# Seven-product pairs in the mixing stages of a two-layer encoder

## The chip, the cores and the metric

The kernel runs on one core of a Trainium2 chip. The metric is the device time of one execution in microseconds; the kernel before takes 1991.8 us, the median of three runs (1990.81, 1991.8, 1995.55). The engines are TensorE (PE, with PEld for its weight loads), VectorE (DVE), ScalarE (ACT), GpSimd (POOL) and SyncE (SP), which only issues transfers.

## The reference

Two layers work on 256 tokens of width 2048, in float32. With the parts that do not matter here left out:

```python
for l in range(DEPTH):                       # DEPTH = 2
    h = rms_norm(x, g_mix[l])
    z = h @ w_in[l]
    # layer 0: z = u (1536), v (1536), memory queries (512): gelu, spatial gating u * s(v)
    # layer 1: z = q (1536), k (512), v (512), memory queries (512): attention with axial rotary
    kv = rms_norm(mem, g_mem[l]) @ w_mem_kv[l]           # 512 keys and 512 values for 256 memory tokens
    x = x + concatenate([tok_out, mem_out]) @ w_out[l]   # 2048 x 2048
    gate, up = split(rms_norm(x, g_ffn[l]) @ w_gate_up[l])   # 2048 x 2 * 5632
    x = x + (silu(gate) * up) @ w_down[l]                # 5632 x 2048
```

## The kernel before, in words

**Products.** Each float32 operand is split into a rounded half `hi` and a residue `lo`; `matmul3` (L187, L188, L189) forms a product as three PE instructions on 128x512 pieces. Activations are kept transposed as `hi` and `lo` in a `Parts` table, 128 features by 128 tokens each. Weights arrive by transfers on SP into `raw` tiles (four of them, 128x2048), and `halves` makes `whi` on ACT (L271) and `wlo` on DVE (L272), three buffers each.

**Two schemes.** `Linear` computes 512 output columns for both token halves: 16 row blocks by 2 token halves by 3 instructions, 96 in all, in two output banks; one `tick` comes for every two row blocks, eight in all. `Pair` computes two neighbouring blocks of 512 columns at once in eight units, each of two row blocks by two token halves by two column blocks. A unit is done by `eight` (24 instructions) or by `seven`, a seven-product scheme (21 instructions). `seven` needs sums of the four weight pieces (L380, L381, L382 in `prepare`, into a tile `T`, and the residue of `T` in a second call of `halves`) and sums of the activations (`feature_sums`, `activation_sums`, L324 to L331). The products 1, 5, 6, 7 of all the sevens are collected in four banks of the room's own, which `inner` adds up into `E` after the last seven (L434 to L437); the products 2, 3, 4, 8 have the four banks of `psa`, which `outer` adds to that at the end (L458). A unit makes two ticks, a pair 16.

**Order.** The program is written as one sequence; `later(n, f)` puts a piece of work n ticks ahead, `tick` runs what is due. From that sequence a planner with a time model fixes each engine's order of instructions. Activations to be transposed go through `turned`: a copy that separates 16-bit planes (L200), a transposing transfer on ACT's queue (L201), and a copy that joins them (L206), after which `split` makes `hi` and `lo` (L181, L182).

**Stages.** Layer 0 mixes first: v in three blocks, the memory queries, `w_mem_kv` keys and values, u in three blocks, then the four blocks of `w_out` with `add_residual` (L658), all by `Linear`. Meanwhile the gates, the memory's norm and the four memory heads (`attend`: `queries`, `scores`, `turn`, `weigh`) run from `later`. Layer 1 mixes likewise with keys, values, three query blocks with attention, memory queries, memory keys and values, and `w_out`. Between lies the feed-forward: three chunks (four, four and three blocks of 512 hidden columns), each with its gate/up pairs, two or three sevens in eight units, and then two `w_down` pairs, with up to three. The mixing stage of a layer has a room of 36 tiles of 128x512 (`big`) and four single banks; the feed-forward has 26 tiles, two `T` buffers, `E`, and the four banks as two double ones.

## Time and profile before

| | |
|---|---|
| median of three runs | 1991.8 us (1990.81 to 1995.55) |
| the profiled execution | 1994.35 us, its span 1992.6 us |
| PE, DVE, ACT, POOL busy | 99%, 83%, 61%, 4% of the span |
| 128x512 products | 8457 of PE's 8913 instructions |
| read from HBM | 394.45 MB |
| granted clock of PE | 0.999 as a mean |

PE's busy time is the union of its instructions, and these overlap: what a product costs is read from the number of products in a stretch that PE fills. A stage is a stretch of the span; the view of windows gives the busy time of every engine in it.

### The profile page before, as it was taken

The numbers are of one execution on the slowest core, as the hardware profiler recorded it, in microseconds if no ns is written. First come the engines' busy times: TensorE is split into PE (matmuls) and PEld (weight loads), VectorE is DVE, ScalarE is ACT, GpSimd is POOL, SyncE is SP. The second block draws the span as 40 slices with busy tenths as digits, with TensorE's granted clock in tenths as the row PEclk, the third lists the DMA queues.
The fourth block names the chain that finished last, engine by engine and source line by source line (L and its number), as shares of the span: only waits on it lengthen the run. The fifth ranks groups of instructions, "written<-read, shape, count | busy, mean of one in ns | idle before, by whom it ended". The sixth has DMA issues, their size and how long they took to land.

```text
span 1992.6 us, 24068 instructions
## 1 busy us (share of the span) xinstructions
PE 1980.8 (99%) x8913; PEld 1640.5 (82%) x8913; DVE 1649.1 (83%) x1783; ACT 1214.7 (61%) x1461; POOL 80.1 (4%) x122
## 2 busy tenths in 40 slices
PE   9999999999999999999999999999999999999998
PEld 7888888888888888888888888888888888888877
...
GB/s 348 300 190 227 217 213 188 194 227 205 232 240 181 231 212 240 233 186 226 250 200 210 154 148 158 216 166 230 224 201 248 198 216 236 199 249 196 223 212 125
DMA packets 283494, 425.93 MB, mean 214 GB/s; under 512 B 89680, under 2 KB 89936, under 8 KB 283376
## 3 DMA queue, kind: packets, MB, share of 16 engines
...
q14 instruction: 48, 0.39, 0.1%
HBM read 394.45 MB, written 2.10 MB: 199 GB/s over the span
## 4 chain that ended last, share of the span: by engine, by line
PE 92%; DMA 3%; DVE 2%; ACT 2%; issue 1%; SPq 0%; ACTq 0%; DVEq 0%
PE acc L189 26%; PE acc L187 26%; PE acc L188 26%; PE m L187 4%; PE m L189 4%; PE m L188 4%; DMA a<-a 2%; DVE wlo L272 1%; DMA raw<-in_w_in_a 1%; ACT whi L271 1%; PE m L193 0%; DVE T L380 0%; PE m L561 0%; PE m L698 0%; ACT junk L213 0%
## 5 line engine op out<-in xcount | busy, mean ns | idle before, releaser
L272 DVE TENSOR_TENSOR wlo<-raw,whi 128x2048 fp32r<-128x2048 f32 (+2 forms) x466 | 840.8, 1821 | 209.5 <-ACT whi L271 203.3
L271 ACT CAST whi<-raw 128x2048 fp32r<-128x2048 f32 (+2 forms) x466 | 705.8, 1535 | 445.8 <-PE acc L188 313.5
L187 PE MATMUL acc<-whi,h 128*128 128x512 f32 x1440 | 561.2, 390 | 0.8 <-ACT whi L271 0.8
L188 PE MATMUL acc<-whi,h 128*128 128x512 f32 x1440 | 560.7, 389 | 0.0
L189 PE MATMUL acc<-wlo,h 128*128 128x512 f32 x1440 | 514.4, 390 | 0.2
L187 PE MATMUL acc<-whi,a 128*128 128x512 f32 x999 | 389.3, 390 | 3.5 <-ACT a L181 3.4
L188 PE MATMUL acc<-whi,a 128*128 128x512 f32 x999 | 389.7, 390 | 0.0
L189 PE MATMUL acc<-wlo,a 128*128 128x512 f32 x999 | 366.7, 391 | 0.8 <-DVE wlo L272 0.7
L189 PEld LDWEIGHTS acc<-wlo,h 128*128 128x128 f32 x1440 | 270.3, 188 | 57.8 <-DVE wlo L272 2.1
L187 PEld LDWEIGHTS acc<-whi,h 128*128 128x128 f32 x1440 | 270.5, 188 | 56.6 <-ACT whi L271 1.4
L188 PEld LDWEIGHTS acc<-whi,h 128*128 128x128 f32 x1440 | 270.4, 188 | 55.6
L187 PEld LDWEIGHTS acc<-whi,a 128*128 128x128 f32 x999 | 187.9, 188 | 42.7 <-ACT a L181 3.9
L189 PEld LDWEIGHTS acc<-wlo,a 128*128 128x128 f32 x999 | 187.8, 188 | 41.7 <-DVE wlo L272 2.8
L188 PEld LDWEIGHTS acc<-whi,a 128*128 128x128 f32 x999 | 188.0, 188 | 38.9
L271 ACT CAST whi<-T 128x1536 fp32r<-128x1536 f32 x93 | 137.8, 1481 | 122.6 <-PE acc L188 103.3
L272 DVE TENSOR_TENSOR wlo<-T,whi 128x1536 fp32r<-128x1536 f32 x93 | 162.9, 1751 | 1.8 <-ACT whi L271 1.8
L380 DVE TENSOR_TENSOR T<-raw 128x1024 f32<-128x1024 f32 x93 | 113.4, 1220 | 20.6 <-DMA raw<-in_w_gate_up 20.4
L187 PE MATMUL m<-whi,a 128*128 128x512 f32 x284 | 110.7, 390 | 0.0
L188 PE MATMUL m<-whi,a 128*128 128x512 f32 x284 | 110.5, 389 | 0.0
L189 PE MATMUL m<-wlo,a 128*128 128x512 f32 x284 | 110.5, 389 | 0.0
L458 DVE TENSOR_TENSOR e<-acc,e 128x512 f32<-128x512 f32 x120 | 78.8, 684 | 2.0 <-PE acc L189 1.7
L206 ACT COPY sg<-a 128x1024 uint16<-128x1024 uint16 x44 | 51.5, 1171 | 33.1 <-DMA a<-a 32.8
(145 smaller groups left out, 1517.7 us busy)
## 6 DMA issues: line engine op xcount, KB each, us to landing
...
```

The source lines that it names most:

```text
L187: nc.tensor.matmul(out, lhsT=a[0], rhs=b[0], start=start, stop=False)
L188: nc.tensor.matmul(out, lhsT=a[1], rhs=b[0], start=False, stop=False)
L189: nc.tensor.matmul(out, lhsT=a[0], rhs=b[1], start=False, stop=stop)
L206: copy(halves, back.rearrange("p (h n) -> p n h", h=2))
L271: nc.scalar.copy(hi[:, cut], raw[:, cut])
L272: nc.vector.tensor_tensor(lo[:, cut], raw[:, cut], hi[:, cut].bitcast(F32), ALU.subtract)
L380: nc.vector.tensor_tensor(T[:, :2], raw[:, 1:4:2], w01, ALU.add)
L458: nc.vector.tensor_tensor(o[t][n], self.bank[name], o[t][n], op)
```

## The change

Six pairs of linear blocks become `Pair`s in which units 0 and 1 have seven products: v blocks 1 and 2, memory keys and values of layer 0, u blocks 0 and 1, keys and values of layer 1, and blocks 0 and 1 of `w_out` in both layers (`two`). The activation sums come from `block_sums`, put ahead with `sums_later`; the first of them in three places uses the `T` buffer as scratch (`apart`). Layer 0's room has 29 tiles beside one `T` and one `E`; in layer 1 the sums lie in separate tiles (`loose`) of `big` or `kept`. The four banks change between single and double with `open_banks`. The first v block is copied out of its banks. The memory heads of layer 0 run later (waits 4, 30, 34, 40 for 4, 16, 20, 28), the u blocks' plane copies go from DVE to ACT, and layer 1's keys are turned later. In the last chunk of `w_down` the seven-product units stand one or two places later, and the last activations are collected three ticks after their transfer for two. `feature_sums` gives way to `block_sums`, which does the same.

```diff
...
 KC4 = 4
-MIX_TILES = 36
+MIX_TILES = (29, 36)
 FFN_TILES = 26
...
     def __init__(self):
-        self.ap, self.whole = {}, {}
+        self.ap, self.whole, self.pair = {}, {}, {}
...
-    def open_rooms(scope, name, tiles, banks):
+    def open_rooms(scope, name, tiles, banks, scratch=2):
         room["p"] = scope.enter_context(tc.tile_pool(name=name, bufs=tiles, reuse_waits="tile"))
-        room["m"] = scope.enter_context(tc.tile_pool(name=f"ps_{name}", bufs=4 // banks, space=PS))
+        room["scratch"] = scratch
+        open_banks(name, banks)
+    def open_banks(name, banks):
+        close_banks()
+        room["psum"] = ExitStack()
+        room["m"] = room["psum"].enter_context(tc.tile_pool(name=nm(f"ps_{name}"), bufs=4 // banks, space=PS))
         room["banks"] = banks
+    def close_banks():
+        if "psum" in room:
+            room.pop("psum").close()
...
-    def split(src, shape):
-        hi = big(F32R, shape)
-        lo = big(F32R, shape)
+    def split(src, shape, tiles=None):
+        hi, lo = [(tiles or big)(F32R, shape) for _ in range(2)]
         nc.scalar.copy(hi, src)
...
                 parts.put(2 * i + c, t, hi[:, c, ts], lo[:, c, ts])
+        parts.pair[i] = hi, lo
...
             nc.vector.tensor_tensor(lo[:, cut], raw[:, cut], hi[:, cut].bitcast(F32), ALU.subtract)
+        return [(hi[:, c, :], lo[:, c, :]) for c in range(n)]
+    def single_halves(raws):
+        n = len(raws)
+        hi = wp.tile([P, KC4, NB], F32R, tag="whi", name=nm("whi"))[:, :n]
+        lo = wp.tile([P, KC4, NB], F32R, tag="wlo", name=nm("wlo"))[:, :n]
+        for c, raw in enumerate(raws):
+            nc.scalar.copy(hi[:, c], raw)
+            nc.vector.tensor_tensor(lo[:, c], raw, hi[:, c].bitcast(F32), ALU.subtract)
         return [(hi[:, c, :], lo[:, c, :]) for c in range(n)]
...
-    def activation_sums(a0, a1, apart=False):
+    def activation_sums(a0, a1, apart=False, tiles=None):
         if apart:
-            q = room["p"].tile([P, KC3, NB], F32, tag="T", name=nm("T"), bufs=2)[:, 0].rearrange("p (c n) -> p c n", n=P)
+            q = room["p"].tile([P, KC3, NB], F32, tag="T", name=nm("T"), bufs=room["scratch"])[:, 0].rearrange("p (c n) -> p c n", n=P)
         else:
-            q = big(F32, [P, 4, P])
+            q = (tiles or big)(F32, [P, 4, P])
         nc.vector.tensor_tensor(q[:, 0], a1[:, 0], a1[:, 1], ALU.subtract)
...
         else:
-            hi, lo = split(q, [P, 4, P])
+            hi, lo = split(q, [P, 4, P], tiles)
         return [(hi[:, i, :], lo[:, i, :]) for i in range(4)]
...
-        def __init__(self, parts, sums, w, na, nb, order, fast, into=None, onto=None):
+        def __init__(self, parts, sums, w, na, nb, order, fast, into=None, onto=None, loose=None):
             self.parts, self.sums, self.w, self.na, self.nb = parts, sums, w, na, nb
-            self.into, self.onto = into, onto
+            self.into, self.onto, self.loose = into, onto, loose
             self.bank, self.two, self.part, self.ready = {}, {}, {}, {}
...
             if i in self.fast:
-                T = room["p"].tile([P, KC3, NB], F32, tag="T", name=nm("T"), bufs=2)
-                w01 = raw[:, 0].unsqueeze(1).to_broadcast([P, 2, NB])
-                nc.vector.tensor_tensor(T[:, :2], raw[:, 1:4:2], w01, ALU.add)
-                nc.vector.tensor_tensor(raw[:, 0], T[:, 0], raw[:, 3], ALU.add)
-                nc.vector.tensor_tensor(T[:, 2], raw[:, 0], raw[:, 2], ALU.add)
+                if self.loose:
+                    T = [self.loose(F32, [P, NB]) for _ in range(KC3)]
+                    for c in range(2):
+                        nc.vector.tensor_tensor(T[c], raw[:, 1 + 2 * c], raw[:, 0], ALU.add)
+                else:
+                    T = room["p"].tile([P, KC3, NB], F32, tag="T", name=nm("T"), bufs=room["scratch"])
+                    w01 = raw[:, 0].unsqueeze(1).to_broadcast([P, 2, NB])
+                    nc.vector.tensor_tensor(T[:, :2], raw[:, 1:4:2], w01, ALU.add)
+                t0, t2 = (T[0], T[2]) if self.loose else (T[:, 0], T[:, 2])
+                nc.vector.tensor_tensor(raw[:, 0], t0, raw[:, 3], ALU.add)
+                nc.vector.tensor_tensor(t2, raw[:, 0], raw[:, 2], ALU.add)
                 self.ready[i] = raw, T
...
             t2, w00, w10, w11 = halves(raw, KC4)
-            t1, t3, t4 = halves(T, KC3)
+            t1, t3, t4 = single_halves(T) if self.loose else halves(T, KC3)
             get, (q5, s2, q7, q3) = self.parts.get, self.sums[i]
...
             b = self.bank
+            if self.loose:
+                e = [self.loose(F32, [P, NB]) for _ in range(4)]
+                nc.scalar.copy(e[0], b[1])
+                nc.vector.tensor_tensor(e[3], b[6], e[0], ALU.subtract)
+                for one, name in ((1, 5), (2, 7)):
+                    nc.vector.tensor_tensor(e[one], b[name], e[3], ALU.add)
+                nc.vector.tensor_tensor(e[3], b[5], e[2], ALU.add)
+                self.out = [[e[2 * t + n] for n in range(2)] for t in range(NT)]
+                return
             E = room["p"].tile([P, 4, NB], F32, tag="e", name=nm("e"), bufs=1)
...
             hi, lo = split(po.rearrange("p (h s) -> p h s", h=2), [P, 2, S])
+            parts.pair[kc0 // 2 + pr] = hi, lo
             for hh in range(2):
...
-        def keys(self):
-            acc = linear(self.parts, w_mem_kv[self.l], 0)
+        def keys(self, acc=None):
+            acc = acc or linear(self.parts, w_mem_kv[self.l], 0)
             kn = head_norm(acc, self.r, ghead[f"mk{self.l}"])
...
-        def values(self):
-            self.V = scaled(linear(self.parts, w_mem_kv[self.l], NB), self.r)
+        def values(self, acc=None):
+            self.V = scaled(acc or linear(self.parts, w_mem_kv[self.l], NB), self.r)
...
+    def block_sums(parts, i, apart=False, tiles=None):
+        whole = []
+        for t in range(NT):
+            if i in parts.pair:
+                both = [a[:, :, t * P:(t + 1) * P] for a in parts.pair[i]]
+            else:
+                both = [a[:, 2 * (i % 2):2 * (i % 2) + 2] for a in parts.whole[i // 2, t]]
+            a = (tiles or big)(F32, [P, 2, P])
+            nc.vector.tensor_tensor(a, both[0].bitcast(F32), both[1].bitcast(F32), ALU.add)
+            whole.append(a)
+        return activation_sums(*whole, apart, tiles)
+    def two(parts, sums, w, n0, order, fast, loose=None):
+        g = Pair(parts, sums, w, n0, n0 + NB, order, fast, loose=loose)
+        g.run()
+        return [[g.out[t][n] for t in range(NT)] for n in range(2)]
+    def sums_later(parts, sums, i, wait, apart=False, tiles=None):
+        def make():
+            sums[i] = block_sums(parts, i, apart, tiles)
+        later(wait, make)
     hT = Parts()
...
         scope = ExitStack()
-        open_rooms(scope, f"mix{l}", MIX_TILES, 1)
+        open_rooms(scope, f"mix{l}", MIX_TILES[l], 2, 1)
         cat = Parts()
         m = Memory(l)
+        hsums, msums, csums = {}, {}, {}
         if l == 0:
...
                     hi, lo = split(whole, [P, 4, P])
+                    cat.whole[c, t] = hi, lo
                     for i in range(4):
...
-                turned(us, 3, parts, True, nc.vector.tensor_copy)
+                turned(us, 3, parts, True)
...
                 for t in range(NT):
-                    v[t][c] = big()
+                    v[t][c] = acc[t] if not c else big()
                     nc.scalar.activation(v[t][c], acc[t], AF.Gelu, scale=norm.r[t])
...
-            later(7, lambda: gated(0, acc))
-            for c in (1, 2):
-                gated(c, linear(hT, w, TOK + c * NB))
+            whole = [big() for _ in range(NT)]
+            for t in range(NT):
+                nc.vector.tensor_copy(whole[t], acc[t])
+            later(7, lambda: gated(0, whole))
+            for i in range(2):
+                sums_later(hT, hsums, i, 1 + 2 * i, not i)
+            for c, acc_c in zip((1, 2), two(hT, hsums, w, TOK + NB, (2, 3, 0, 4, 1, 5, 6, 7), (0, 1))):
+                gated(c, acc_c)
+            open_banks("mix0", 1)
             for t in range(NT):
...
                     later(3 + 3 * t + c, lambda t=t, c=c: gate(t, c))
-            m.attend(linear(hT, w, 2 * TOK), norm.r, cat, (4, 16, 20, 28), True)
-            m.keys()
-            m.values()
+            for i in range(2):
+                sums_later(m.parts, msums, i, 4 + 2 * i, not i)
+            m.attend(linear(hT, w, 2 * TOK), norm.r, cat, (4, 30, 34, 40), True)
+            open_banks("mix0", 2)
+            keys, values = two(m.parts, msums, w_mem_kv[0], 0, (2, 3, 4, 0, 5, 1, 6, 7), (0, 1))
+            open_banks("mix0", 1)
+            m.keys(keys)
+            m.values(values)
+            open_banks("mix0", 2)
+            for i in range(2):
+                sums_later(hT, hsums, i, i, not i)
+            blocks = two(hT, hsums, w, 0, (2, 3, 0, 4, 1, 5, 6, 7), (0, 1))
             for c in range(3):
-                acc = linear(hT, w, c * NB)
+                acc = blocks[c] if c < 2 else linear(hT, w, c * NB)
+                if c == 2:
+                    for i in range(2):
+                        sums_later(cat, csums, i, 1 + 2 * i)
                 for t in range(NT):
...
             m.prep(20, 2)
-            acc = linear(hT, w, TOK)
+            for i in range(2):
+                sums_later(hT, hsums, i, 1 + 2 * i)
+            acc, values = two(hT, hsums, w, TOK, (2, 3, 4, 0, 5, 1, 6, 7), (0, 1), big)
+            open_banks("mix1", 1)
             kn = head_norm(acc, norm.r, ghead["k"], True)
...
-            later(7, turn_k)
-            own["v"] = scaled(linear(hT, w, TOK + MEMW), norm.r)
+            own["v"] = scaled(values, norm.r)
+            later(3, turn_k)
             for c in range(3):
...
         units = kd if l else [(12, KC4), (0, KC4), (4, KC4), (8, KC4)]
+        if l:
+            for i in range(2):
+                sums_later(cat, csums, i, 1 + 2 * i, tiles=kept)
+            later(6, lambda: open_banks("mix1", 2))
+            blocks = two(cat, csums, w_out[l], 0, (2, 3, 4, 0, 5, 1, 6, 7), (0, 1), kept)
+        else:
+            blocks = two(cat, csums, w_out[l], 0, (2, 3, 0, 1, 6, 7, 4, 5), (0, 1))
         for j in range(4):
-            acc = linear(cat, w_out[l], j * NB, units)
+            acc = blocks[j] if j < 2 else linear(cat, w_out[l], j * NB, units)
             add_residual(acc, j, norm, gslice("ffn", l), hF, j < 3, nc.scalar.copy if l else nc.vector.tensor_copy)
+        close_banks()
         room.clear()
...
-        def feature_sums(i):
-            j, c = i // 2, 2 * (i % 2)
-            whole = []
-            for t in range(NT):
-                hi, lo = hF.whole[j, t]
-                a = big(F32, [P, 2, P])
-                nc.vector.tensor_tensor(a, hi[:, c:c + 2].bitcast(F32), lo[:, c:c + 2].bitcast(F32), ALU.add)
-                whole.append(a)
-            sums[i] = activation_sums(*whole)
         for i in fast:
-            later(2 + 2 * i, lambda i=i: feature_sums(i))
+            sums_later(hF, sums, i, 2 + 2 * i)
...
                     nc.vector.scalar_tensor_tensor(a, g.out[t][1], norm.r[t], a, ALU.mult, ALU.mult)
-                    wait, ticks = (3, 2) if f == chunk[-1] else (11, 3)
+                    wait, ticks = (3, 3 if last else 2) if f == chunk[-1] else (11, 3)
                     later(wait + t, lambda a=a, t=t, f=f, ticks=ticks: turn_a(a, t, f, ticks))
...
                 for n, i in enumerate(some):
-                    order.insert((0, 2, 4 + (not jj))[n], i)
+                    order.insert(1 + n + jj if last else (0, 2, 4 + (not jj))[n], i)
                 into = [Columns(X2[t][jj]) for t in range(NT)] if last else None
...
         norm = next_norm
+        close_banks()
         room.clear()
...
     flush()
```

## The prediction

> **What bounds the kernel now.** I first read the page's busy shares and the list of what TensorE (PE) waited for.
>
> ```profile
> PE 1980.8 (99%) x8913; PEld 1640.5 (82%) x8913; DVE 1649.1 (83%) x1783; ACT 1214.7 (61%) x1461; POOL 80.1 (4%) x122
> ```
>
> ```profile
> PE acc L187 <- ACT a L181: 3.4, 1, 3.4
> ```
>
> PE is busy for all but 12 us of the span of 1992.6 us, and the longest of its waits is one of 3.4 us. A PE that does not wait is shortened only by taking products away; so the question is what one product costs, and whether VectorE (DVE), the next engine at 83%, can deliver the operands of the new scheme in time. Both are read stage by stage. I found the stages on the timeline by counting 128x512 products in program order: a linear block of 512 columns has 96, a pair with two seven-product units 186, with three 183.
>
> ```profile
> core 0: us, PE busy (x) PEld busy (x) DVE busy (x) ACT busy (x) POOL busy (x), PEclk, DMA share, GB/s
> 28.79:73.83 45.04, 44.15 (x194) 35.88 (x193) 23.42 (x25) 34.82 (x76) 16.50 (x39) 1.00 1.02 362
> 73.83:100.90 27.07, 27.07 (x145) 23.29 (x144) 21.39 (x35) 22.16 (x59) 9.43 (x16) 1.00 0.69 235
> 100.90:216.81 115.91, 115.27 (x531) 95.77 (x530) 85.18 (x126) 63.90 (x109) 3.69 (x4) 1.00 0.70 206
> 144.52:170.37 25.85, 25.21 (x121) 20.73 (x120) 23.17 (x40) 16.77 (x33) 0.00 (x0) 1.00 0.64 185
> 216.81:238.57 21.76, 21.76 (x97) 18.02 (x96) 15.40 (x18) 10.07 (x13) 0.00 (x0) 1.00 0.73 218
> 216.81:303.85 87.04, 87.04 (x385) 72.07 (x384) 61.30 (x81) 46.47 (x83) 0.00 (x0) 1.00 0.71 217
> 303.85:346.96 43.11, 43.11 (x196) 35.70 (x194) 39.63 (x55) 23.43 (x31) 5.96 (x4) 1.00 0.56 190
> 994.94:1063.04 68.10, 68.10 (x314) 56.46 (x312) 43.68 (x69) 38.90 (x79) 6.61 (x11) 1.00 0.61 198
> 1199.74:1294.43 94.69, 94.69 (x449) 79.40 (x448) 59.18 (x85) 64.68 (x117) 0.00 (x0) 1.00 0.63 190
> 1337.55:1379.14 41.59, 41.59 (x185) 34.21 (x183) 39.54 (x38) 28.84 (x24) 0.00 (x0) 1.00 0.67 216
> 1940.44:1944.49 4.05, 0.62 (x4) 0.19 (x2) 4.05 (x5) 2.76 (x4) 0.00 (x0) 1.00 0.72 219
> 1944.49:1948.85 4.36, 4.36 (x13) 3.43 (x14) 4.36 (x5) 1.75 (x1) 0.00 (x0) 0.66 0.88 262
> ```
>
> In order, the rows are: v blocks 1 and 2; the query block with the gates; memory keys, values and the three u blocks; the first u block alone; the first block of w_out; all of w_out of layer 0; the first gate/up pair; keys, values and first query block of layer 1; its whole w_out; a later gate/up pair; and two pieces of the last chunk of w_down. The row of the first w_out block gives the price of a product: 96 in 21.76 us is **0.2267 us** from start to start (the 0.39 us that a product's own group shows overlaps its neighbours). The first gate/up pair is the model for the change, 186 products of which two units have seven: 186 x 0.2267 = 42.16, and its row lasts 43.11 with eight transposes among them, so the pair scheme as such, started behind a linear block, costs PE nothing extra. The gate/up row at 1337.55 shows DVE busy 39.54 of 41.59 us, **95%**, without a PE wait. The mixing stages of before have shown less: 23.17 of 25.85, 90%, in the first u block, with 0.64 us of PE idle.
>
> **The change, part by part.**
>
> *Products.* Six pairs of linear blocks (v 1 and 2, u 0 and 1, memory keys and values, layer 1's keys and values, w_out blocks 0 and 1 of each layer) get two seven-product units each. A unit of eight is 24 PE instructions, of seven 21. So 6 x 2 x 3 = 36 products go: 36 x 0.2267 = **-8.16 us**. No transposes are added. This is the ceiling of the main part.
>
> *DVE work that the pairs add.* These are the groups by line and shape that carry the prices:
>
> ```profile
> L272 DVE TENSOR_TENSOR wlo<-raw,whi 128x2048 fp32r<-128x2048 f32 x264 | 603.4, 2288 | 118.0 <-ACT whi L271 113.3 <-DMA a<-a 4.4
> L272 DVE TENSOR_TENSOR wlo<-raw,whi 128x1024 fp32r<-128x1024 f32 x198 | 234.8, 1221 | 91.2 <-ACT whi L271 89.8 <-PE m L193 0.7
> L272 DVE TENSOR_TENSOR wlo<-T,whi 128x1536 fp32r<-128x1536 f32 x93 | 162.9, 1751 | 1.8 <-ACT whi L271 1.8
> L271 ACT CAST whi<-T 128x1536 fp32r<-128x1536 f32 x93 | 137.8, 1481 | 122.6 <-PE acc L188 103.3 <-DVE T L382 16.1 <-PE m L188 3.2
> L380 DVE TENSOR_TENSOR T<-raw 128x1024 f32<-128x1024 f32 x93 | 113.4, 1220 | 20.6 <-DMA raw<-in_w_gate_up 20.4
> L458 DVE TENSOR_TENSOR e<-acc,e 128x512 f32<-128x512 f32 x120 | 78.8, 684 | 2.0 <-PE acc L189 1.7
> L381 DVE TENSOR_TENSOR raw<-T,raw 128x512 f32<-128x512 f32 x93 | 63.6, 684 | 0.0
> L436 DVE TENSOR_TENSOR e<-m,e 128x1024 f32<-128x1024 f32 x33 | 40.2, 1218 | 0.1
> L437 DVE TENSOR_TENSOR e<-m,e 128x512 f32<-128x512 f32 x33 | 22.6, 685 | 0.1
> L182 DVE TENSOR_TENSOR a<-a,a 128x512 fp32r<-128x512 f32 x27 | 18.3, 684 | 1.4 <-ACT a L181 1.4
> L206 DVE COPY a<-a 128x1024 uint16<-128x1024 uint16 x20 | 13.9, 694 | 16.2 <-DMA a<-a 15.7
> L200 DVE COPY a<-a 128x1024 uint16<-128x1024 uint16 x14 | 9.5, 687 | 0.1
> L324 DVE TENSOR_TENSOR a<-a 128x128 f32<-128x128 f32 x17 | 4.8, 285 | 0.9 <-ACT a L852 0.9
> L831 DVE TENSOR_TENSOR a<-h,h 128x256 f32<-128x256 f32 x12 | 4.5, 418 | 0.0
> ```
>
> Per pair, with the same-shaped neighbours of a row at its price: the residues of the weights in 8 pieces of 2.288 instead of 16 of 1.221, -1.23; two units' sums of weights with their residue, 2 x (1.220 + 0.684 + 0.684 + 1.751) = 8.68; the inner sum, 0.685 + 1.218 + 0.685 = 2.59; four outer additions, 4 x 0.684 = 2.74; two sets of activation sums, 2 x (2 x 0.418 + 4 x 0.285 + 0.684) = 5.32. Together **18.1 us**. In layer 1 the sums lie in separate tiles, so each 1024-wide operation becomes two of 0.684 and the 1536-wide residue three of the same: 2 x (0.15 + 0.30) + 0.15 more, 19.2. ACT gets 2 x 1.481 and small casts, some 3 us a pair, and the u blocks' 12 copies that DVE gives up; the tightest of its stages, the query block, leaves it 27.07 - 22.16 = 4.9. The doubled number of weight transfers issued by SP (two halves for a unit) delays nothing that PE waits for in the gate/up pairs, where it is so already.
>
> *DVE against PE, by stage.* v: 23.42 + 18.1 + two copies of the first block at 0.684 = 42.9, against a PE stage of 45.04 - 6 x 0.2267 = 43.7: 98%. Query block, into which the memory pair's activation sums fall: 21.39 + 5.3 = 26.7 of 27.07: 99%. Memory pair and u: 85.18 + 2 x 18.1 - 5.3 - 4 x (0.687 + 0.694) for the copies that go to ACT = 110.6 of 115.91 - 2.72 = 113.2: 98%. w_out of layer 0: 61.30 + 18.1 - 2.8 = 76.6 of 85.7: 89%. Layer 1's keys to first query: 43.68 + 19.2 = 62.9 of 66.7: 94%. Its w_out: 59.18 + 19.2 = 78.4 of 93.3: 84%. No stage asks for more DVE than it has PE time; three ask for more than the 95% seen without a wait. If 100% is usable the price is 0. If 95% is: v 42.9 / 0.951 = 45.1, +1.4; query 28.1, +1.0; memory and u 116.3, +3.1; **5.5 us** in all. Layer 0's room also shrinks from 36 tiles to 29; whatever waits for a tile waits on DVE, ACT or a transfer, and so is part of this price. The memory heads' scores, turns and weighing move past the pair into u and the first tick of w_out; they keep their price and stay in the row 100.90 to 216.81. I take 2.0, nearer the lower end, since the added instructions are the gate/up pairs' own and the program can lay them beside the slacker neighbours.
>
> *One buffer and the banks.* Layer 0's mixing room has one T buffer where the feed-forward has two. Where two seven-product units follow each other (w_out of layer 0) the second's sums start when the first's residue is made: 1.220 + 0.684 + 0.684 of sums and a cast of its weights (1.481 even for the narrower T) against the four products, 12 x 0.2267 = 2.72, still in hand: 0 to 1.8 us late, once hidden if another unit is drawn forward. In front of the memory pair, its third and fourth output banks are those that the query block's norm still reads; three units' first halves, 36 x 0.2267 = 8.2 us, stand before them, so I bound this at 0 to 2 us. Both together 0 to 3.8; I take 1.0.
>
> *Transfers in v.* The v row has the DMA engines busy all the time at 362 GB/s. If this cannot rise, v does not get shorter and 6 x 0.2267 = 1.4 us of the saving stays behind; this is inside the 5.5 above. The Trainium skill ("Perfetto Trace Analysis", Roofline) puts one core's practical ceiling at about 435 GB/s for its 16 DMA engines; by it v would not be transfer-bound, and this price would be 0. The row's share of 1.02 speaks against that much room.
>
> *The last chunk.* Here a seven-product unit no longer comes first, and the last activation is collected one tick later. The chain of waits tells what this touches:
>
> ```profile
> 1922.59 0.63 ACT sg L871
> 1923.22 0.92 issue
> 1924.14 0.64 ACT whi L271
> 1924.78 1.18 issue
> 1925.96 1.48 ACT whi L271
> 1927.44 0.95 ACT a L200
> 1928.41 6.76 DMA a<-a
> 1935.20 7.40 DMA a<-a
> 1942.62 1.18 ACT sg L206
> 1943.82 0.63 ACT a L181
> 1944.49 0.74 PE acc L187 x2
> ```
>
> Two transposing transfers, one after the other, decide when PE can go on. The first starts behind the copy at 1927.44, and that copy stood from 1924.14 behind two weight casts, the second of them (1.48) that of T for the second seven-product unit; both were let in because the first unit, of seven products, had given its two weight buffers back. With an eight-product unit first, one buffer comes back, and 3 products later; so I expect the copy and the transfers up to 1927.44 - 1924.14 = 3.3 us earlier. PE's own work ahead of the wait stays 90 products. What is lost now is the idle 3.4 and then a slow clock: the last row of the stages, 1944.49 to 1948.85, shows a granted clock of 0.66, (1 - 0.66) x 4.36 = 1.5. So the gain is bounded by -3.4 - 1.5 = -4.9; the other bound is that the later tick only delays the collecting copy by half a unit, 12 x 0.2267 = +2.7. I take **-3.0**. Layer 0's last chunk, whose order moves the same way, is not among PE's longer waits.
>
> The Trainium skill ("TensorE: Matmul & The Clock Gate", Part 1) says that an idle window of about 3.4 us halves the clock until as long a busy one has passed. The 0.66 behind the 3.4 us wait agrees. By that rule even a slightly shorter wait saves the whole slow stretch, and the term would be -3.0 - 1.5, the total 1.5 us lower.
>
> *Sum.* -8.16 + 2.0 + 1.0 - 3.0 = **-8.2 us**. The profiled execution took 1994.35 us for its span of 1992.6, so it would become 1986.2; it lies 2.6 above the median of 1991.8, and the forecast for the median is 1991.8 - 8.2 = **1984 us**.
>
> **The rivals.**
>
> *A: the saving is eaten half.* DVE at 95% (5.5) and the buffers at 1.9 with the last chunk as before: -8.2 + 7.4 = -0.8, 1991; with the last chunk's -3.0, 1988. For it: three stages at 98%, with bursts (softmax, norm) that the gate/up pairs do not have. Against it: the 95% without any wait.
>
> *B: slower.* DVE becomes the bound of layer 0's mixing stages, because DVE and ACT take their work in order and a weight residue stands behind a norm, a softmax or a transfer's copy; PE waits for the residue. The point is the usable DVE share. At the 90% of the first u block: v 47.7, +4.0; query 29.7, +2.6; memory and u 122.9, +9.7; layer 1's keys to query 69.9, +3.2: 19.5 us. With -8.2 and no gain in the last chunk this is +11.3, **2003 us**. It turns slower than before below about 94% (8 us lost). For it: the only stage of mixing as full as that did wait 0.64 us. Against: those 0.64 us are what 90% cost there, far from 10%.
>
> *C: the pairs work and the last chunk does not move.* -8.2 + 3.0 = -5.2: 1987. For it: the two transfers, 14.2 us, are longer than all that stands in front of them, and a weight load sharing the queue sets them.
>
> **How the numbers follow.** Less than 0.3% (6 us) either way I call no change. Forecast 0.52 (its own range 1978 to 1986), A 0.20, C 0.15, B 0.13. Part of A's and C's mass lies just under the bound and of the forecast's just over it: faster 0.55, same 0.33, slower 0.12. The lower end is all saved and no price, -8.2 - 4.9 = -13.1, 1978.7; the upper must take A wholly and the start of B: 1997.
>
> **What would show it.** PE instructions fall by 36 x 1 to 8877, and the six pair stages last 42.2 us plus what is between their units. Right: PE busy near 1973 and no new line among PE's waits over 3 us in total. The last chunk is right if its first transposing transfer starts within 3 us of the silu (1922.59 to 1928.41 is 5.8 now) and the clock behind it stays at 1.00. Wrong: PE waiting for L272 or for the sums' lines in v, the query block, or u (A, B), DVE at 97% or more there beside PE idle of microseconds; or the 3.4 us wait unchanged (C).

## The result and the profile after

The changed kernel takes **2042.5 us**, the median of its runs (2037.3 to 2045.7); the kernel before took 1991.3 us beside it. The ratio is **1.0245, with a 95% interval of 1.0230 to 1.0259**: 49 us slower where 8 us faster was forecast. The profiled execution took 2044.65 us, its span is 2042.8 us, 50.2 more than before. Of the executions behind the ratios in this document one is not counted, of 5176 us among twelve of the kernel with the v pair alone.

The busy shares of the changed kernel:

```profile
PE 1986.2 (97%) x8877; PEld 1636.6 (80%) x8877; DVE 1739.1 (85%) x1913; ACT 1252.7 (61%) x1463; POOL 92.3 (5%) x122
```

The 36 products are gone (8913 to 8877 instructions), yet PE, idle for 12 us of the span before, is idle for 57 now. What it waited for, as total, number of times and longest:

```profile
PE acc L197 <- ACT a L191: 19.0, 1, 19.0
PE m L197 <- ACT whi L282: 16.6, 6, 9.3
PE acc L199 <- DVE wlo L283: 3.3, 9, 0.9
PE m L596 <- ACT junk L503: 2.5, 1, 2.5
PE acc L197 <- DVE x L493: 1.2, 1, 1.2
```

Two waits, of 19.0 and 9.3 us, are more than half of the loss. (In the changed kernel's numbering L197 to L199 are the products, L282 and L283 the weight halves, L191 and L192 `split`, L210, L211 and L216 the plane copy, the transposing transfer and the joining copy.) I counted products as in the prediction to find the stages, and took the view of windows for the pairs of layer 0:

```profile
core 0: us, PE busy (x) PEld busy (x) DVE busy (x) ACT busy (x) POOL busy (x), PEclk, DMA share, GB/s
28.60:75.67 47.07, 43.72 (x188) 34.22 (x186) 39.18 (x49) 37.93 (x74) 29.65 (x43) 1.00 1.00 346
102.86:246.65 143.79, 112.86 (x496) 91.24 (x494) 110.14 (x148) 77.47 (x107) 5.13 (x5) 0.91 0.62 177
149.14:205.00 55.86, 46.58 (x206) 38.39 (x206) 46.08 (x68) 29.43 (x47) 1.84 (x2) 0.91 0.54 178
205.00:246.65 41.65, 22.64 (x104) 18.52 (x102) 25.51 (x35) 24.74 (x31) 0.00 (x0) 0.82 0.78 168
246.65:250.50 3.85, 3.85 (x10) 3.17 (x11) 3.85 (x7) 3.07 (x6) 0.00 (x0) 0.50 0.47 167
246.65:346.14 99.49, 94.58 (x402) 77.56 (x403) 75.77 (x105) 57.79 (x94) 0.00 (x0) 0.94 0.60 176
```

In order: the v pair; the memory pair with all of u; the u pair alone; the last u block; the first products of w_out; all of w_out. By the same counting the parts of the kernel went, before to after: mixing of layer 0 from 297.1 to 339.5 us, feed-forward 691.1 to 692.6, mixing of layer 1 299.5 to 305.5, feed-forward up to the two `w_down` pairs of its last chunk 625.6 to 630.0, these two pairs 72.5 to 68.6. So **42 of the 50 us were lost in layer 0's mixing**, 6 in layer 1's, and the last chunk gained 3.9. Of the 5.9 in the feed-forward, 2.4 are in layer 1's first gate/up pair (45.5 us for 43.1); in all kernels with layer 1's w_out pair it takes 44.2 to 45.5, in the others 43.1. The rest says little: over the profiled executions of the kernels below the feed-forward of layer 0 varies from 689.5 to 697.7 us.

**The 19.0 us wait** stands at 227, in front of w_out. ACT's timeline of the changed kernel there (start, duration, what; in brackets the idle time ahead and what ended it):

```profile
210.30 0.48 ACT L574 ACTIVATE a<-m,s 128x256 f32<-128x256 f32 x1 [2.40 <-DVE s L570]
212.64 2.57 ACT L866 ACTIVATE a<-e,s 128x512 f32<-128x512 f32 x4
217.01 1.04 ACT L210 COPY a<-a 128x1024 uint16<-128x1024 uint16 x1
218.08 1.25 ACTq L211 DMA_TRANSPOSE a<-a  x1
...
230.25 1.05 ACT L210 COPY a<-a 128x1024 uint16<-128x1024 uint16 x1 [5.76 <-issue]
235.14 1.05 ACT L210 COPY a<-a 128x1024 uint16<-128x1024 uint16 x1 [2.78 <-issue]
243.33 0.62 ACT L191 CAST a<-a 128x512 fp32r<-128x512 f32 x1 [5.35 <-issue]
245.98 1.14 ACT L191 CAST a<-a 128x512 fp32r<-128x512 f32 x2
```

Both u blocks are ready at 205, at the pair's end, but their activation (L866) comes behind the memory heads' softmax (L574), which stands in u now, and their first transposing transfer starts at 218.08, 13 us later. Eight such transfers are then due, four of u and four of the heads, and with them come the first weights of w_out. The windows of the changed kernel in which PE runs out, and its DMA view from 218 to 240 (queues with packets, MB and the share of 16 engines; issues with KB each and median time to landing):

```profile
223.40:236.00 12.60, 4.24 (x19) 3.19 (x17) 3.52 (x3) 4.06 (x4) 0.00 (x0) 0.82 1.11 260
236.00:241.00 5.00, 0.00 (x0) 0.00 (x0) 1.68 (x3) 1.98 (x2) 0.00 (x0) 0.50 1.20 122
```

```profile
q1 hardware_dynamic: 1632, 3.15, 53.4%
q10 hardware_dynamic: 5956, 1.48, 52.4%
...
raw<-in_w_out SPq DMA_DIRECT2D x6, 512.0 KB, 8.4
a<-a ACTq DMA_TRANSPOSE x6, 7.8
```

DVE works for 5.2 and ACT for 6.0 of these 17.6 us, about a third, and **the DMA engines are full** by the view's share (1.11 and 1.20): half of it is the weights' queue, half the transposing transfers'. Summaries of these transfers, first of the changed kernel between 200 and 250, then of the kernel before from the memory keys to the end of w_out (100 to 330), as shortest, median and longest time from issue to landing:

```profile
DMA to landing us min/median/max: 3.1/5.8/13.2
```

```profile
DMA to landing us min/median/max: 3.1/3.7/8.9
```

The longest of the kernel before, 8.9, is one of four issued between 111 and 136, beside the memory keys and values; in its u and w_out none takes over 5.8. The eight of the changed kernel take from 218.1 to 245.1 (the last is issued at 242.0 and lands in 3.1), and ACT stands idle on "issue" for 5.8, 2.8 and 5.4 us meanwhile, so that the plane copies of the next ones come later still. PE had only the last u block, 21.8 us, to cover the 40 us from the pair's end.

**The 9.3 us wait** stands at 160, in front of the u pair's first seven. DVE's timeline of the changed kernel, then ACT's:

```profile
148.90 1.88 DVE L493 TENSOR_TENSOR e<-acc,e 128x512 f32<-128x512 f32 x3
155.39 0.36 DVE L509 TENSOR_SCALAR s<-s,mem_r 128x4 f32<-128x4 f32 x2 [4.61 <-POOL s L185]
159.08 1.43 DVE L709 TENSOR_TENSOR a<-h,h 128x256 f32<-128x256 f32 x4
164.43 1.22 DVE L405 TENSOR_TENSOR T<-raw 128x1024 f32<-128x1024 f32 x1
166.88 0.69 DVE L408 TENSOR_TENSOR T<-raw 128x512 f32<-128x512 f32 x1
```

```profile
161.96 0.62 ACT L350 CAST sg<-T 128x512 fp32r<-128x512 f32 x1 [7.39 <-DVE T L347]
167.61 1.90 ACT L282 CAST whi<-raw 128x2048 fp32r<-128x2048 f32 x1 [4.51 <-DVE T L408]
```

The memory pair ends at 149. The keys' norm (squares on ACT, a power on POOL) stands next in DVE's order, and DVE is idle 4.6 us for it; then come the activation sums (L709), the weight sums (L405, L408), and only at 167.61 the cast for which PE waits. DVE is busy 82% of this stage. It was idle while the work that PE would need lay behind a norm in its queue.

### The profile page after: what moved, and what is told of

Same layout as the page of the kernel before. It is cut to its first block, busy times and chain, and to the rows that moved or that the text cites. A ratio compares the mean times of both kernels' runs of the same rounds, so it can differ in the third digit from the quotient of the medians.

```text
span 2042.8 us, 24271 instructions
## 1 busy us (share of the span) xinstructions
PE 1986.2 (97%) x8877; PEld 1636.6 (80%) x8877; DVE 1739.1 (85%) x1913; ACT 1252.7 (61%) x1463; POOL 92.3 (5%) x122
## 4 chain that ended last, share of the span: by engine, by line
PE 75%; DVE 7%; DMA 4%; ACT 3%; issue 2%; ACTq 0%; POOL 0%; SPq 0%; DVEq 0%
PE acc L199 21%; PE acc L197 21%; PE acc L198 21%; PE m L197 4%; PE m L198 4%; PE m L199 4%; DVE wlo L283 3%; DMA a<-a 3%; ACT whi L282 2%; DVE T L405 1%; DMA raw<-in_w_gate_up 1%; DMA raw<-in_w_down 1%; PE m L203 0%; ACT a L210 0%; DVE raw L407 0%
## 5 line engine op out<-in xcount | busy, mean ns | idle before, releaser
L282 ACT CAST whi<-raw 128x2048 fp32r<-128x2048 f32 (+2 forms) x418 | 703.1, 1693 | 466.0 <-PE acc L198 329.2
L283 DVE TENSOR_TENSOR wlo<-raw,whi 128x2048 fp32r<-128x2048 f32 (+2 forms) x418 | 838.5, 2014 | 166.4 <-ACT whi L282 161.9
L198 PE MATMUL acc<-whi,h 128*128 128x512 f32 x1406 | 548.3, 390 | 1.8 <-DVE h L242 1.8
L197 PE MATMUL acc<-whi,h 128*128 128x512 f32 x1406 | 548.7, 390 | 1.2 <-ACT whi L282 1.1
L199 PE MATMUL acc<-wlo,h 128*128 128x512 f32 x1406 | 497.1, 390 | 2.6 <-DVE wlo L283 2.6
L197 PE MATMUL acc<-whi,a 128*128 128x512 f32 x970 | 380.2, 393 | 22.3 <-ACT a L191 19.0
L198 PE MATMUL acc<-whi,a 128*128 128x512 f32 x970 | 379.8, 392 | 0.0
L199 PE MATMUL acc<-wlo,a 128*128 128x512 f32 x970 | 351.6, 391 | 0.9 <-DVE wlo L283 0.7
L199 PEld LDWEIGHTS acc<-wlo,h 128*128 128x128 f32 x1406 | 264.0, 188 | 60.3 <-DVE wlo L283 5.9
L197 PEld LDWEIGHTS acc<-whi,h 128*128 128x128 f32 x1406 | 264.3, 188 | 56.5 <-ACT whi L282 2.0
L198 PEld LDWEIGHTS acc<-whi,h 128*128 128x128 f32 x1406 | 264.2, 188 | 56.4 <-DVE h L242 2.2
L197 PEld LDWEIGHTS acc<-whi,a 128*128 128x128 f32 x970 | 183.2, 189 | 62.2 <-ACT a L191 19.4
L282 ACT CAST whi<-T 128x1536 fp32r<-128x1536 f32 x101 | 149.8, 1483 | 115.0 <-PE acc L198 88.7
L199 PEld LDWEIGHTS acc<-wlo,a 128*128 128x128 f32 x970 | 183.2, 189 | 40.8 <-DVE wlo L283 3.0
L283 DVE TENSOR_TENSOR wlo<-T,whi 128x1536 fp32r<-128x1536 f32 x101 | 177.3, 1756 | 7.7 <-PE acc L199 4.7
L405 DVE TENSOR_TENSOR T<-raw 128x1024 f32<-128x1024 f32 x101 | 123.5, 1223 | 19.0 <-DMA raw<-in_w_gate_up 18.6
L197 PE MATMUL m<-whi,a 128*128 128x512 f32 x311 | 122.6, 394 | 5.7 <-ACT whi L282 5.5
L199 PE MATMUL m<-wlo,a 128*128 128x512 f32 x311 | 121.7, 391 | 1.0 <-DVE wlo L283 1.0
L198 PE MATMUL m<-whi,a 128*128 128x512 f32 x311 | 121.8, 392 | 0.0
L493 DVE TENSOR_TENSOR e<-acc,e 128x512 f32<-128x512 f32 x136 | 89.9, 690 | 1.4 <-PE acc L199 0.9
L197 PEld LDWEIGHTS m<-whi,a 128*128 128x128 f32 x311 | 58.7, 189 | 20.6 <-ACT whi L282 8.9
```

The lines of the kernel that those rows point to most:

```text
L197: nc.tensor.matmul(out, lhsT=a[0], rhs=b[0], start=start, stop=False)
L198: nc.tensor.matmul(out, lhsT=a[1], rhs=b[0], start=False, stop=False)
L199: nc.tensor.matmul(out, lhsT=a[0], rhs=b[1], start=False, stop=stop)
L282: nc.scalar.copy(hi[:, cut], raw[:, cut])
L283: nc.vector.tensor_tensor(lo[:, cut], raw[:, cut], hi[:, cut].bitcast(F32), ALU.subtract)
L405: nc.vector.tensor_tensor(T[:, :2], raw[:, 1:4:2], w01, ALU.add)
```

## The experiments

The time differences below are the ratio less 1, times the median of the kernel before beside which the run stood (1990.9 to 1998.4).

**Taking parts out of the changed kernel.** First the u blocks linear again:

```diff
-            for i in range(2):
-                sums_later(hT, hsums, i, i, not i)
-            blocks = two(hT, hsums, w, 0, (2, 3, 0, 4, 1, 5, 6, 7), (0, 1))
...
-                acc = blocks[c] if c < 2 else linear(hT, w, c * NB)
+                acc = linear(hT, w, c * NB)
```

> The changed kernel with the three u blocks as linear blocks again, everything else as changed (waits of the heads, copies on ACT, w_out pair). Theory 'crowd': the two longest waits, 9.4 us in the u pair and 19.2 us in front of w_out, come from the u pair alone, because both u blocks become ready at once and their four transposing transfers fall together with the four of the memory heads. Then both waits and their slow clock go, some 34 us, six products of 0.2267 come back: about 2042 - 34 + 1 = 2009 us. Theory 'DVE bound': 18 us of DVE work go from a stage in which DVE is 98% full, so at most about that much time comes back and the wait in front of w_out stays over 10 us: 2024 us or more.

Measured: 1.0115 (1.0095 to 1.0134), +23 us for +49. Of PE's waits in this kernel:

```profile
PE m L197 <- ACT whi L282: 4.6, 1, 4.6
PE acc L197 <- ACT a L191: 3.8, 1, 3.8
```

These are all over 0.5 us between 150 and 320. Taking out the u pair gives back 26 of the 49 us, between the 33 of 'crowd' and the 18 of 'DVE bound'. The 9.3 and 19.0 us waits are gone, but the w_out pair still takes 55.3 us, where two linear blocks took 43.5: about half the loss does not hang on the u pair.

Then the first two blocks of w_out linear again, reading the u blocks first and the heads third:

```diff
-            blocks = two(cat, csums, w_out[l], 0, (2, 3, 0, 1, 6, 7, 4, 5), (0, 1))
+            blocks = []
...
-        units = kd if l else [(12, KC4), (0, KC4), (4, KC4), (8, KC4)]
+        units = kd if l else [(4, KC4), (0, KC4), (12, KC4), (8, KC4)]
```

> The changed kernel with the first two w_out blocks of layer 0 as linear blocks, in the same order of row blocks as the pair (4, 0, 12, 8); u pair kept. Theory 'crowd': the 19 us in front of w_out stay, since the first rows wanted are still u block 1; the 4.5 us wait before the first seven-product unit and its slow clock (some 7 us) go: about 2042 - 7 + 1 = 2036 us. Theory 'DVE bound': with 18 us of DVE work less the wait in front of w_out shrinks by more than half: 2025 us or less.

Measured: 1.0178 (1.0159 to 1.0196), +35.5 us. 13 us come back, again between the two forecasts. The wait in front of w_out is still 14.1 us, so the pair there does not make most of it.

Then the heads turned by transposes on PE, so that four of the eight transfers go:

```diff
-                if dma:
+                if False:
```

> The changed kernel with the memory heads' four softmax blocks of layer 0 transposed by PE (16 transposes, 1.7 us of PE) instead of by four transposing transfers; the u blocks' transfers stay. Theory 'crowd': eight transfers at 3.4 us one after the other become four, so the wait in front of w_out falls from 19 to about 6 us: 2042 - 13 + 2 = 2031 us. Theory 'DVE bound': DVE gives up eight plane copies (5.5 us) only: 2037 us or more and the wait stays over 12 us.

Measured: 1.0152 (1.0128 to 1.0175), +30 us, 18 less than the change. The two longest waits of this kernel:

```profile
PE m L197 <- ACT whi L282: 12.3, 5, 9.2
PE m L197 <- DVE a L192: 7.0, 1, 7.0
```

The wait in front of w_out goes from 19.0 to 7.0 and the w_out pair from 56.0 to 43.0 us. **The crowd of transposing transfers is shown as the cause of most of this wait**; the 9.2 in u is untouched. The edit takes away with the four transfers their issues on ACT and their plane copies, so whether the full DMA engines or ACT, which stands idle at its issues, set the pace is not separated.

Then the heads two and three ticks later still:

```diff
-            m.attend(linear(hT, w, 2 * TOK), norm.r, cat, (4, 30, 34, 40), True)
+            m.attend(linear(hT, w, 2 * TOK), norm.r, cat, (4, 30, 37, 42), True)
```

> The changed kernel with the memory heads' turn three ticks later (37 for 34) and the weighing two (42 for 40), so that the four transposing transfers of u blocks 0 and 1 come before the heads' four. Theory 'crowd': what delays the u blocks is the heads' transfers in front of them, four at some 3.4 us; the wait in front of w_out falls from 19 to about 6 us and the time to about 2029 us. Theory 'late start': the u blocks are late because the softmax and the gelus stand in ACT's order after the pair's end and the first transfer starts 13 us after it; then the wait stays at 14 us or more and the time at 2037 or more.

Measured: 1.0229 (1.0207 to 1.025). The waits of this kernel from 200 to 320:

```profile
PE m L197 <- ACT a L191: 5.5, 1, 5.5
PE acc L197 <- ACT a L191: 4.2, 1, 4.2
```

The 19.0 became 4.2 in front of the pair, and 5.5 and smaller ones inside it, where the pair took 63.1 us for 56.0. The wait fell as 'crowd' said and the time stayed as 'late start' said: the work was pushed on, not away.

Then the u pair's sevens one unit later:

```diff
-            blocks = two(hT, hsums, w, 0, (2, 3, 0, 4, 1, 5, 6, 7), (0, 1))
+            blocks = two(hT, hsums, w, 0, (2, 3, 4, 0, 5, 1, 6, 7), (0, 1))
```

> The changed kernel with the u pair's seven-product units one place later, order 2, 3, 4, 0, 5, 1, 6, 7 as in the memory pair. Theory 'sums behind the norm': the 9.4 us wait before the first seven-product unit of u comes from its activation sums and weight sums standing in DVE's order behind the memory keys' norm, which waits for GpSimd; one eight-product unit more in front (24 products, 5.4 us) takes 5 us off it and, the idle being under 4 us, its slow clock of 1.6 us: 2042 - 7 = 2035 us. Theory 'DVE bound': the DVE work before that point grows by one residue of 2.3 us, so only 3 us come off and the wait stays over 6: 2038 us or more.

Measured: 1.0217 (1.0196 to 1.0239). The wait fell from 9.3 to 5.6 us and the u pair from 55.8 to 52.1; a full unit of 24 products (5.4 us) in front did not cover it: 3.7 us came off, between the 5 and the 3 of the two theories.

**Layer 1.** The change without layer 1's two pairs, and layer 1's two pairs alone:

```diff
-            acc, values = two(hT, hsums, w, TOK, (2, 3, 4, 0, 5, 1, 6, 7), (0, 1), big)
+            acc = linear(hT, w, TOK)
...
-            blocks = two(cat, csums, w_out[l], 0, (2, 3, 4, 0, 5, 1, 6, 7), (0, 1), kept)
+            blocks = []
```

> The changed kernel with layer 1's two pairs (keys and values, w_out) as linear blocks. The stages of layer 1's mixing lasted 305.5 us in the changed kernel against 299.5 before, so if they lose on their own account, this gives back 6 us there and some 2 in the gate/up stage behind: 2034 us. If the loss in layer 1 only follows from what layer 0 did to the order, it gives back nothing: 2042 us or, with four products' units lost, 2045.

Measured: 1.0197 (1.018 to 1.0214).

```diff
 # the kernel before, and
+            acc, values = two(hT, hsums, w, TOK, (2, 3, 4, 0, 5, 1, 6, 7), (0, 1), big)
...
+            blocks = two(cat, csums, w_out[l], 0, (2, 3, 4, 0, 5, 1, 6, 7), (0, 1), kept)
```

> The kernel before with layer 1's two pairs alone; layer 0 and the last chunk as before. 12 products of 0.2267 go, 2.7 us. If these pairs lose on their own account, the mixing stage takes 305.5 us as in the changed kernel and the time is 6 to 8 us above before, 1999 us. If a pair costs nothing when the stages before it are undisturbed: 2.7 us below before, 1988.5 us.

Measured: 1.0052 (1.0037 to 1.0067), +10 us. Both runs put layer 1's pairs at about 10 us of the 49. The largest piece is the memory keys' stretch, 33.8 us for 30.3; of PE's waits in it:

```profile
PE m L596 <- ACT junk L503: 2.5, 1, 2.5
```

**Each pair by itself.** Each kernel is the one before with one pair of the change; for layer 1 the lines above, for the others these. The kernels with a pair of layer 0 alone also have the change's room of 29 tiles, and **those of the u pair and of the w_out pair alone have u's plane copies on ACT**, as in the change, so what they lose is the loss of the pair and of that move together. The smaller room by itself is no great part: in the kernel of the v pair the stages behind the pair last as before but for the first two u blocks (52.1 us for 50.5), and in that of the w_out pair all stages in front of the pair do.

```diff
+            for c, acc_c in zip((1, 2), two(hT, hsums, w, TOK + NB, (2, 3, 0, 4, 1, 5, 6, 7), (0, 1))):   # v
+            keys, values = two(m.parts, msums, w_mem_kv[0], 0, (2, 3, 4, 0, 5, 1, 6, 7), (0, 1))        # memory
+            blocks = two(hT, hsums, w, 0, (2, 3, 0, 4, 1, 5, 6, 7), (0, 1))                             # u
+            blocks = two(cat, csums, w_out[l], 0, (2, 3, 0, 1, 6, 7, 4, 5), (0, 1))                     # w_out
```

> The kernel before with the seven-product pair of v alone; everything else as before. Theory, each pair's loss is made in its own stretch by the order of the work on ACT and DVE: the v pair is 2.0 us longer than the two linear blocks in the changed kernel's trace (45.04 to 47.07), the query 0.1: +2 us over before, within 1 us. Rival, a pair alone is sound and only the crowd of pairs makes the waits: 6 products fewer, -1.4 us.

Measured: 1.0016 (1.0006 to 1.0025), +3 us; the pair lasts 47.1 us, as in the change.

> The kernel before with the pair of the memory's keys and values alone (and the heads' waits of the change, since the pair has ticks of its own). Theory, loss made in its own stretch: the memory pair is 2.7 us longer in the changed kernel (43.62 to 46.27): +2 to +4 us. Rival, a pair alone is sound: -1.4 us. If the memory pair's norm is what makes the 9.4 us wait of the u stretch, a wait of some us appears here at the start of u too, although u is linear, and the loss goes over 5 us.

Measured: 1.0048 (1.0036 to 1.006), +9.6 us. The pair lasts 46.0 for 43.6, but no wait appears at the start of u, which is 4.0 us shorter; 10.6 us are lost at the last u block and the first of w_out. So the bet on the pair's norm failed for a linear u.

> The kernel before with layer 1's keys/values pair alone. Theory, both blocks come out together and the heads' norm and softmax behind them fall on one stretch: the loss of layer 1's two pairs (11.1 us) is mostly here, in the memory keys' stretch behind (30.30 to 33.79 there): +5 to +8 us, with that stretch over 33 us. Rival, the loss is that of the w_out pair: within 1.5 us of before here, and the memory keys' stretch at 30 to 31.

Measured: 0.9993 (0.9981 to 1.0005): the only pair that costs nothing, and it gains nothing either. The memory keys' stretch stays at 30.2. The bet that it loses 5 to 8 us failed.

> The kernel before with layer 1's w_out pair alone. Theory, loss with the keys/values pair: within 2.5 us above before (0.9 us in the pair, 1.1 us in the first feed-forward stretch behind it in the run of layer 1's two pairs). Rival, the loss of layer 1 is that of the w_out pair and of what comes behind it: +7 us or more.

Measured: 1.0012 (1.0003 to 1.0021), +2.4 us. The two pairs of layer 1 cost +1 us apart and +10 together; in the run of both the softmax (L574) in the memory keys' stretch starts 23.6 us into it instead of 18.6, and runs among the keys' squares (L503). Why the planner orders it so was not tried.

> The kernel before with layer 0's u pair alone (heads at their old waits; the plane copies of u on ACT as in the change). Theory, the 9.4 us wait in the u pair comes from the memory pair in front of it, whose norm and whose sums fill DVE and ACT there, and the 19.2 us wait from eight transposing transfers together: here only u's own four are late, so the u stretch has no wait over 3 us and the wait in front of w_out is some 2 to 5 us; time within +6 us of before. Rival, the u pair loses by itself: both blocks' transfers come out at once and the first unit waits, +15 us or more.

Measured: 1.0086 (1.0066 to 1.0106), +17 us, **the dearest pair, and by itself**. So my theory fell that this wait needs the memory pair in front; the rival's size is right, but not its place. Two views of this kernel, PE's waits and the window that ends with the longest of them:

```profile
PE m L197 <- ACT whi L282: 10.2, 2, 7.9
```

```profile
158.00:166.10 8.10, 1.85 (x9) 1.19 (x7) 7.45 (x18) 1.52 (x3) 0.00 (x0) 0.89 0.23 43
```

While PE waits, DVE is busy for 7.45 of 8.10 us. Its timeline there shows with what:

```profile
154.58 0.74 DVE L631 SCALAR_TENSOR_TENSOR a<-acc,mem_r,a 128x512 fp32r<-128x512 f32 x1
157.50 0.76 DVE L709 TENSOR_TENSOR a<-h,h 128x256 f32<-128x256 f32 x2
159.04 0.61 DVE L579 TENSOR_SCALAR a<-a,s 128x256 f32<-128x256 f32 x2
160.62 1.22 DVE L405 TENSOR_TENSOR T<-raw 128x1024 f32<-128x1024 f32 x1
164.16 0.69 DVE L408 TENSOR_TENSOR T<-raw 128x512 f32<-128x512 f32 x1
```

Softmax (L579), the memory values (L631), the activation sums (L709) and the heads' plane copies share DVE with the weight sums of the first seven (L405, L408). At the heads' old place the u pair has too much DVE work for some 10 us. In the changed kernel, with the heads later, the pair takes 55.8 us for the 61.9 here, and the block behind it loses 19.9 us where it loses nothing here. No run has the u pair with the heads later and linear memory blocks.

> The kernel before with layer 0's w_out pair alone. Theory: the pair begins with units of the second u block, which a linear u delivers 22 us before w_out, and its heads are done at their old waits; loss within 3 us of before, in the first seven of the pair (4.5 us waited there in the changed kernel, behind ACT's copies) and in its inner sums. Rival, one T buffer and the order 2, 3, 0, 1 lose by themselves what the changed kernel's w_out pair shows beside the weighing (43.52 to 53): +7 us or more.

Measured: 1.0035 (1.002 to 1.005), +7 us, at the rival's bound. The pair lasts 49.9 us for 43.5. The wait and ACT's timeline of this kernel:

```profile
PE m L197 <- ACT whi L282: 4.1, 1, 4.1
```

```profile
227.08 1.17 ACT L216 COPY a<-a 128x1024 uint16<-128x1024 uint16 x1 [3.47 <-DMA a<-a]
228.44 1.48 ACT L282 CAST whi<-T 128x1536 fp32r<-128x1536 f32 x1 [0.18 <-ACT a L216]
```

T had its sums at 211; its cast stands in ACT's order behind the joining copy of the last u block, which waits 3.5 us for a transposing transfer. That copy is on ACT only by the move of u's plane copies, which this kernel takes over from the change.

**The heads' move and its cure.** The kernel before with only the heads' later places, and the memory pair with the heads' turns on PE:

```diff
-            m.attend(linear(hT, w, 2 * TOK), norm.r, cat, (4, 16, 20, 28), True)
+            m.attend(linear(hT, w, 2 * TOK), norm.r, cat, (4, 30, 34, 40), True)
```

> The kernel before with no pair, only the memory heads' waits of the change (4, 30, 34, 40 for 4, 16, 20, 28): their transposing transfers then fall beside those of u. Theory, in the run of the memory pair alone (+9.6 us) the loss at u's last block and w_out's first (8.5 and 2.1 us over the products) is that of the heads: here too, +6 to +10 us. Rival, the pair's sums and norm make it: within 2 us of before here.

Measured: 1.0021 (1.0009 to 1.0034), +4 us: 8.2 and 2.3 us lost at u's last block and w_out's first, the place and size of the memory pair's run, and 4.1 gained in u's first. The net is under what I expected, since I had left that gain out.

```diff
 # the memory pair alone, and
-                if dma:
+                if False:
```

> The kernel before with the memory pair alone, as in the run of that pair, but the heads' turns done as transposes on PE, so no transfer of theirs. Theory: the 10.6 us lost at u's last block and w_out's first go but for the transposes' own 2 us or so; the pair's own 2.4 us and the 4 us gained in u's first block stay: between -2 and +3 us of before. Rival, the loss is not that of the transfers: +7 us or more.

Measured: 1.002 (1.0007 to 1.0033), +4 us for the memory pair's 9.6; u's last block and w_out's first lose 5.6 for 10.6. About half of the loss was that of the transfers.

**The last chunk and attempts to mend.** The kernel before with only the later places in the last chunks:

```diff
-                    order.insert((0, 2, 4 + (not jj))[n], i)
+                    order.insert(1 + n + jj if last else (0, 2, 4 + (not jj))[n], i)
```

> The kernel before with the last-chunk part of the change alone (seven-product units one or two places later, collecting copy one tick later); no mixing pair is changed. If that part worked on its own, the last w_down stage shortens as in the changed kernel (36.6 to 32.7 us) and the time is 1987 us, 4 below before. If its gain in the changed kernel was only chance of placement, it stays within 1 us of before, 1991.

Measured: 0.9998 (0.9985 to 1.001). The two last w_down pairs took 69.6 us for 72.5 in the profiled execution. Over all kernels profiled here they took 69.3 on average with the changed places (9 kernels, 68.4 to 71.2) and 71.3 with the old (11, 69.4 to 72.6): a gain of about 2 us, which the time of this run could not show.

```diff
-            blocks = two(cat, csums, w_out[l], 0, (2, 3, 0, 1, 6, 7, 4, 5), (0, 1))
+            blocks = two(cat, csums, w_out[l], 0, (6, 7, 2, 0, 3, 1, 4, 5), (0, 1))
```

> The kernel before with layer 0's w_out pair alone, as in the run of that pair, but its units in the order 6, 7, 2, 0, 3, 1, 4, 5: the memory heads first, the seven-product units fourth and sixth instead of third and fourth. Theory, T's cast waits behind the copies of the last transposed block because the first seven comes early, and the second because one T buffer serves both: the 4.1 us wait goes, the pair lasts 43 to 45 us for 49.9, time within 0 to -2 us of before. Rival, the additions on DVE and the inner sum make the loss wherever the sevens stand: still +4 us or more.

Measured: 1.0028 (1.0017 to 1.0039), +5.6 us. The waits left in the pair:

```profile
PE acc L199 <- DVE wlo L283: 1.5, 1, 1.5
PE m L199 <- DVE wlo L283: 1.3, 1, 1.3
```

The 4.1 us wait is gone and the pair lasts 46.2 for 49.9, still above the 43.5 of the linear blocks; in time the intervals of the two orders overlap. Part of the loss is the place of the sevens; the rest stays in this order too. How much of that is the move of u's plane copies the next kernel tells, which has them on DVE.

```diff
 # the kernel before with layer 1's keys/values pair, w_out's in the order above, and the last chunk's places
+            acc, values = two(hT, hsums, w, TOK, (2, 3, 4, 0, 5, 1, 6, 7), (0, 1), big)
+            blocks = two(cat, csums, w_out[l], 0, (6, 7, 2, 0, 3, 1, 4, 5), (0, 1))
+                    order.insert(1 + n + jj if last else (0, 2, 4 + (not jj))[n], i)
```

> The kernel before with layer 1's keys/values pair, layer 0's w_out pair in the order 6, 7, 2, 0, 3, 1, 4, 5, the plane copies of u on DVE as before, and the later places in the last chunks of w_down. 12 products fewer, 2.7 us. If the two pairs and the last chunk are sound where they stand: -2 to -5 us, a ratio of 0.9975 to 0.999. Rival, each further pair only brings new waits: within 1 us of before or slower.

Measured: 1.0024 (1.0013 to 1.0034), +5 us. With u's plane copies on DVE again the w_out pair is down to 43.8 from 46.2, but the first gate/up pair behind it takes 45.7 for 43.1: the two take 89.4 us together, with the copies on ACT 89.3, in the kernel before 86.6. So in these two profiled executions the place of the copies moves the loss and does not make it. The keys/values pair takes 47.7 for 46.3. No version found here beats the kernel before.

**What they add up to.** Alone, v +3.2, memory with its heads +9.6, u +17.2, w_out +7.0, layer 1's two pairs together +10.4, the last chunk -0.4: **+47.0 of +48.8 us**. That this comes out so near is in part luck, and it does not show that the pairs leave each other alone. Layer 1's entry holds both its pairs, which cost +1 apart; u's and w_out's both hold the move of the plane copies; and the losses are not the same ones. The last u block, where the changed kernel loses 19.9 us (41.7 for 21.8), loses nothing with the u pair alone and 8.5 with the memory pair and its heads. What the runs do show is that nearly every pair loses time by itself, that none gains any clear of the noise, and that the waits move from one place to another when pairs stand together.

## Why the prediction was wrong, point by point

**Products: right in number, worth nothing here.** 36 went, as said. But no pair of these runs gained its 1.36 us: layer 1's keys and values alone last 46.4 us for 46.3, and the nearest to a gain is layer 0's w_out pair with the heads turned on PE, 43.0 for 43.5.

**DVE work: right. The step that failed is its price**, "If 100% is usable the price is 0. If 95% is: ... 5.5 us", with 2.0 taken. The forecast gave memory pair and u 110.6 us of DVE; the changed kernel's row 102.86:246.65 has 110.14. It was to fit into 113.2 us at 98%, and took 143.8, at **77%**. A share over a stage of 110 us says only whether the work fits if it may stand anywhere in the stage. What set the time was what stands in front of each operand in the queues of ACT and DVE: a norm in front of the u pair's sums, a joining copy in front of T's cast. The gate/up pairs, from which I took the 95% without a wait, have no norm, softmax or transposed operand due in them. The rows of before had a hint of the difference: 0.64 us of PE idle at 90% in the first u block.

**The moved heads: a second step that failed, costed at nothing.** "They keep their price and stay in the row": their own price stayed, but their four transfers and softmax fell into the stretch of u's. Alone that costs 4 us; in the changed kernel, where both u blocks also come at once, taking the four transfers out saved 18 us of 49. **This term was missing from the sum.** The linear blocks gave each two transfers of u their own 22 us; with the pair, eight have one block as cover, 21.8 us. By an estimate from durations seen here, eight such transfers need from 11.9 us (issued every 1.25, the shortest issue, and 3.1 for the last) to 24.8 (8 x 3.1, one by one), and that without the softmax ahead of them: too near 21.8 to be left out.

**T buffer and banks**, 0 to 3.8 with 1.0 taken: undersized. (The figures of its first part give 2.59 + 1.48 - 2.72 = 1.35 us at most, not 1.8.) The w_out pair alone is 7.7 us over its products, 186 x 0.2267 = 42.2 for 49.9, and its longest wait, 4.1 us, is of a kind that the step did not have: T's cast behind a joining copy on ACT. Drawing other units in between, as the step said, took 3.7 us off. How much of the rest is the one buffer's was not separated.

**Transfers in v:** the row 28.60:75.67 has the DMA engines busy all the time at 346 GB/s, 362 before, and the pair is 2.0 us longer where 1.4 less was hoped for: 3.4 against the 5.5 kept for v and its neighbours. The Trainium skill's ceiling of about 435 GB/s ("Perfetto Trace Analysis", Roofline) was not reached: in both rows the DMA engines are busy all the time well below it. Whether the transfers or the casts (PE waited 1.9 and 1.1 us for L282 there) set the end was not separated.

**The last chunk: right in mechanism, its size about 2 for 3.0.** The first transfer was to start earlier, and it did. ACT's timeline of the changed kernel and the window of this part:

```profile
1975.61 0.72 ACT L951 ACTIVATE sg<-e,s 128x512 f32<-128x512 f32 x1
1977.99 1.25 ACTq L211 DMA_TRANSPOSE a<-a  x1
```

```profile
1974.20:2006.85 32.65, 31.44 (x140) 25.75 (x138) 28.14 (x24) 21.67 (x17) 0.00 (x0) 1.00 0.71 210
```

From the silu to the first transfer it is 2.4 us, for 5.8 and a forecast of 3. The 3.4 us wait for L191 is gone (a wait of 1.2 for L493 follows), and the clock stays at 1.00. In this execution the gain is 3.9 us; over all profiled kernels about 2. The place of the units and the later collecting were not tried apart.

**The rivals.** B, slower by in-order queues on DVE and ACT, named the right mechanism, with 0.13. Its size, +11, failed with its point: it looked for a DVE that is full (94%), and the loss came with DVE at 83% in the v pair, 82% in the u pair and 77% over the memory pair and all of u. What was full was a short window, 92% over the 8.1 us in front of the u pair's first seven in the kernel with that pair alone, and no stage's share shows that. A and C did not come about. C's reason, a weight load that shares the transfers' queue, is not what the DMA view shows: the weights are in q1 and the transposing transfers in q10, and what they share is the 16 engines (53.4% and 52.4%).
